# A streaming encoder layer: the last product as seven block products in a stage of its own

## The chip, the cores and the metric

The kernel runs on one core of one Trainium2 chip. Its time is the device time of one execution in microseconds; the kernel before takes 1970.81 us, the median of three runs (1968.71 to 1971.21). A profile is one further execution, recorded by the hardware. Engines are named as in the profile: PE is the matrix engine and PEld its weight load, DVE the vector engine, ACT the scalar (activation) engine, POOL the general engine, SP the queue that issues the DMAs.

## What is computed

One layer of a hybrid encoder, on 2048 prompt frames and 64 sample frames, with a model width of 1024. Attention with 4 heads (branch A, "diff") and retention with 4 heads (branch B, "ret") each give an output of width 512 per frame. The part that matters here is what follows them:

```python
def layer_output(x, oa, ob, za, zb, ga, gb, subln_g, lam_init, w_oa, w_ob, w_out):
    B, T = x.shape[0], x.shape[1]
    oa = (rmsnorm(oa, subln_g) * (1.0 - lam_init)).reshape(B, T, W_A) * jax.nn.silu(za)
    ob = rmsnorm(ob).reshape(B, T, W_B) * jax.nn.silu(zb)
    m = ga * (oa @ w_oa) + gb * (ob @ w_ob)
    return x + m @ w_out
```

`ga` and `gb` are sigmoids of projected inputs plus a bias. `oa @ w_oa` and `ob @ w_ob` are 512 to 1024 each, and are called the branch products here; `m @ w_out`, 1024 to 1024, is the last product. All inputs and outputs are float32.

## The kernel before, in words

A float32 product is made of three products of a rounded format: each operand is split into a high part (`h`, a cast on ACT) and a low part (`l`, what the cast left out, a subtraction on DVE or POOL), and the sum h·h + h·l + l·h is accumulated in a PSUM bank.

The program is written by a planner. The work is a set of Python generators ("tasks") with priorities; a loop takes the most urgent one that can go on by a model of the engines' times (`P`, `A`, `V`, `G` for PE, ACT, DVE and POOL, `ld` and `st` for DMAs), and the instructions of PE, ACT and DVE stand in exactly the order in which the tasks emit them. Every DMA is issued on SP, in emission order as well. A task that yields a time waits in the model only; on the chip an instruction waits for the data and buffers that it needs. `take` and `give` count buffers of a tag (`BUFS`).

Two streams fill most of the time: input projections (`w_stream`) and attention with retention (`z_stream`). They leave in DRAM the branch outputs (`oaT`, `obT`), the branch gates (`zaT`, `zbT`) and the merge gates before their sigmoid (`gaT`, `gbT`), all transposed, with channels on the partitions, in eight groups of 264 columns (256 prompt frames and 8 sample frames, `GW`).

The last stage (`out_stream`) goes through the eight groups. For a group, `m_tile` makes for each of eight channel tiles (`ct`) the branch product of A in a bank `mm` and of B in a bank `s`, 12 matmuls each with 264 columns (lines 1685 to 1687); `m_fin` multiplies each by its gate (line 1704), adds the two on POOL (1708), splits the sum into high and low tiles that stay in SBUF (1714, 1717), and copies out the sample columns (1723). Then `y_tile` makes the last product of two blocks of 128 frames: for each half of the output channels 24 matmuls with 512 columns (1758 to 1760) into a bank `at`, and `y_fin` adds `x` and stores (1791). The sample frames' product (1754) stands before the last block. `og_fin` makes the operands `ogh`, `ogl` of the branch products: POOL multiplies `on` by `z`, ACT takes the sigmoid of `z`, DVE multiplies by it. `gate` loads `gt` and takes its sigmoid on ACT. `load_wo` and `load_wout` bring the weights and split them.

Of the kernel before, what the change touches and what calls it, by code (L numbers as in the profile page):

```python
# [16 lines left out]
T = 2048  # L17
# [18 lines left out]
        "oz": 11, "og": 16, "gt": 8, "wst": 4, "m": 16, "xt": 2, "yt": 2}  # L36
# [8 lines left out]
EARLY = 3  # L45
# [17 lines left out]
class Hybrid:  # L63
    def __init__(self, tc, ins, outs):
# [9 lines left out]
        self.live = {"z": 0, "w": 0, "r": 0}  # L74
# [80 lines left out]
    def scratch(self):  # L155
# [13 lines left out]
        self.obT = tc.dram_tile([4, 128, 8 * GW], F32, name="obT")  # L169

    def consts(self):
# [33 lines left out]
        nc.vector.tensor_scalar_mul(self.gsub, self.gsub, 0.8)  # L205
# [1201 lines left out]
    def ret_block(self, k, t0, r, first):  # L1407
# [88 lines left out]
        nc.vector.tensor_scalar(ms, ms, 1.0 / 128, EPS, op0=ALU.mult, op1=ALU.add)  # L1496
# [69 lines left out]
    def load_wo(self, q):  # L1566
        sl = slice(256 * q, 256 * q + 256)
        for br, name in enumerate(("w_o_diff", "w_o_ret")):
            for kt in range(4):
                h, l, slot = self.wo[br][kt]  # L1570
                yield from self.take("oz")
                s = self.sb(self.z3, [128, GW], "oz", "wst")[:, :256]
                t = self.ld(s, self.i[name][0, 128 * kt:128 * kt + 128, sl], 1 << 17)
                self.spawn(self.split_fin("oz", h[:, sl], l[:, sl], s, t, (kt + q) % 3 == 0, slot, q), 2)
                yield self.pe

    def load_wout(self):
        pool = self.z4
        for ct in range(8):
            h = pool.tile([128, 1024], F32R, tag=f"woh{ct}", name=f"woh{ct}")  # L1580
            l = pool.tile([128, 1024], F32R, tag=f"wol{ct}", name=f"wol{ct}")
            self.wout.append((h, l, {}))
        for nh in range(2):
            sl = slice(512 * nh, 512 * nh + 512)
            for ct in range(8):
                h, l, slot = self.wout[ct]
                k = 8 * nh + ct
                tag = ("xt", "xt", "yt", "yt")[k] if k < 4 else "wst"
                yield from self.take(tag)
                s = self.sb(pool, [128, 512], tag, "wst")  # L1590
                t = self.ld(s, self.i["w_out"][0, 128 * ct:128 * ct + 128, sl], 1 << 18)
                self.spawn(self.split_fin(tag, h[:, sl], l[:, sl], s, t + 600, False, slot, nh), 2)
                self.wout_left -= 1
                yield self.pe

    def out_prep(self):
        pa = self.z3
        for br, name in enumerate(("w_o_diff", "w_o_ret")):
            for kt in range(4):
                h, l = (pa.tile([128, 1024], F32R, tag=f"{name}{n}{kt}", name=f"{name}{n}{kt}") for n in "hl")  # L1600
                self.wo[br].append((h, l, {}))
        yield from self.load_wo(0)
        for g in range(8):
            gsl = slice(GW * g, GW * g + GW)
            for br, (oT, zT) in enumerate(((self.oaT, self.zaT), (self.obT, self.zbT))):
# [10 lines left out]
            if g == 0:  # L1616
                for ct in range(EARLY):
                    yield from self.take("oz", 2)
                    pair = [self.sb(pa, [128, GW], "oz", "gt") for _ in range(2)]
                    self.spawn(self.gate(ct, pair, "oz"), 1)  # L1620
                for q in range(1, 4):
                    yield from self.load_wo(q)
                yield lambda: self.wout_left == 0

    def og_fin(self, on, z, t, og):
        nc = self.nc
        yield t
        nc.gpsimd.tensor_mul(on, on, z)
        t = self.G(GW, self.pe)
        yield t  # L1630
# [381 lines left out]
```

## Time and profile before

| what | value |
|---|---|
| median of three runs | 1970.81 us |
| profiled execution, first to last instruction | 1970.5 us |
| first branch product (line 1685) | 1588.4 us |
| last matmul ends near | 1966.8 us |
| PE busy | 1954.8 us (99%) |
| DVE, ACT, POOL busy | 1048.8, 993.2, 418.9 us |
| DMA issued on SP | 283.85 MB, 49.0% of the 16 engines' span |

A window row of the profile has, behind its stretch and its length, the busy time of each engine with its number of instructions in brackets, then the granted PE clock as a share, the mean busy share of the 16 DMA engines, and GB/s. A row of the timeline has start, duration, engine, line, operation, tiles and count. A row of a group of instructions has the busy time, the mean duration of one in ns, and then the idle time before them with what ended it. A row of DMA issues has the count, the size of one and the median time from issue to landing.

### The profile page before, as it was taken

How to read it: one execution, taken by the hardware profiler on the slowest of the kernel's cores; microseconds unless marked ns; L12 is line 12 of the kernel's file. 1: busy time of each engine (PE TensorE's matmuls, PEld its weight loads, DVE VectorE, ACT ScalarE, POOL GpSimd, SP SyncE). 2: the span in 40 equal slices, each digit the busy share in tenths (PEclk: the TensorE clock that was granted, in tenths of full speed). 3: DMA queues.
4: the chain of work that ended last, by engine and by line, in shares of the span. 5: the costliest groups of instructions: out<-in, count | busy, mean ns of one | idle time of the engine just before them, and what ended most of it. 6: DMA issues, size and time to landing. Idle time of an engine off the chain costs nothing. (4 is left out here: it accounts for less than half of the span.)

```text
span 1970.5 us, 34013 instructions
## 1 busy us (share of the span) xinstructions
PE 1954.8 (99%) x12158; PEld 1753.9 (89%) x12158; DVE 1048.8 (53%) x2795; ACT 993.2 (50%) x2190; POOL 418.9 (21%) x387
## 2 busy tenths in 40 slices
PE   9999999999999999999999999999999999999999
PEld 7878999999988989999998888888888888888997
DVE  6553665536555236547757656635753356444433
ACT  6432776655544436436756666635654554333321
POOL 2310211212111121212112112112112434222210
PEclk9999999999999999999999999999999999999999
DMA  7647554336655656664352342553234666444432
GB/s 245 212 129 195 152 158 122 110 89 164 180 162 166 163 158 194 189 198 148 105 144 92 97 134 78 160 148 97 65 94 130 197 215 205 145 134 136 140 94 60
DMA packets 332429, 286.03 MB, mean 145 GB/s; under 512 B 65250, under 2 KB 296930, under 8 KB 332259
## 3 DMA queue, kind: packets, MB, share of 16 engines
q1 hardware_dynamic: 332258, 283.85, 49.0%
q8 instruction: 96, 1.57, 0.4%
q14 instruction: 75, 0.61, 0.1%
HBM read 187.22 MB, written 91.49 MB: 141 GB/s over the span
## 5 line engine op out<-in xcount | busy, mean ns | idle before, releaser
L516 PE MATMUL mm<-xh,wh 128*128 128x512 f32 (+2 forms) x1280 | 459.1, 359 | 0.0
L516 PE MATMUL mm<-xh,wl 128*128 128x512 f32 (+2 forms) x1280 | 452.3, 353 | 0.0
L516 PE MATMUL mm<-xl,wh 128*128 128x512 f32 (+2 forms) x1280 | 451.7, 353 | 0.0
L480 POOL TENSOR_TENSOR wl<-ws,wh 128x512 fp32r<-128x512 f32 x189 | 257.0, 1372 | 814.9 <-ACT wh L470 629.5
L516 PEld LDWEIGHTS mm<-xh,wl 128*128 128x128 f32 x1280 | 241.0, 188 | 31.6
L516 PEld LDWEIGHTS mm<-xh,wh 128*128 128x128 f32 x1280 | 241.3, 189 | 29.0 <-issue 0.2
L516 PEld LDWEIGHTS mm<-xl,wh 128*128 128x128 f32 x1280 | 241.6, 189 | 27.9
L516 PE MATMUL mm<-wh,xh 128*128 128x256 f32 (+1 forms) x824 | 258.4, 314 | 1.2 <-DVE tlo L753 1.0
L516 PE MATMUL mm<-wh,xl 128*128 128x256 f32 (+1 forms) x824 | 253.4, 308 | 0.0
L516 PE MATMUL mm<-wl,xh 128*128 128x256 f32 (+1 forms) x824 | 253.1, 307 | 0.1
L1119 DVE TENSOR_TENSOR atl<-at,ath 128x512 fp32r<-128x512 f32 (+1 forms) x144 | 93.8, 660 | 162.6 <-ACT ath L1117 162.6
L810 ACT COPY ev<-mm 128x512 f32<-128x512 f32 x140 | 71.5, 511 | 194.1 <-PE mm L516 166.0
L516 PEld LDWEIGHTS mm<-wh,xh 128*128 128x128 f32 x824 | 156.7, 190 | 10.9 <-DVE tlo L753 1.4
L516 PEld LDWEIGHTS mm<-wl,xh 128*128 128x128 f32 x824 | 156.9, 190 | 9.2 <-POOL wl L480 0.3
L516 PEld LDWEIGHTS mm<-wh,xl 128*128 128x128 f32 x824 | 156.7, 190 | 8.0
L1035 ACT ACTIVATE row<-row,a_mx 128x1024 f32<-128x1024 f32 (+7 forms) x160 | 153.9, 963 | 12.9 <-DVE a_mx L1015 12.6
L1005 DVE CUSTOM_DVE_ANT_0 row<-s,dfar 128x512 f32<-128x512 f32 (+2 forms) x192 | 118.6, 631 | 54.5 <-PE s L997 54.0
L470 ACT CAST wh<-ws 128x512 fp32r<-128x512 f32 x192 | 116.2, 619 | 44.8 <-PE mm L516 18.5
L1117 ACT CAST ath<-at 128x512 fp32r<-128x512 f32 (+1 forms) x144 | 79.0, 564 | 104.8 <-PE at L1104 97.4
L996 PE MATMUL s<-K,q 128*128 128x512 f32 (+3 forms) x320 | 118.7, 374 | 1.4 <-DVE a_acc L1005 1.4
L997 PE MATMUL s<-K,q 128*128 128x512 f32 (+3 forms) x320 | 115.2, 363 | 0.4 <-DMA q<-qT 0.4
L1057 DVE SCALAR_TENSOR_TENSOR row<-row,a_w 128x1024 f32<-128x1024 f32 (+4 forms) x96 | 103.6, 1086 | 14.4 <-ACT row L1054 14.1
(238 smaller groups left out, 4036.1 us busy)
## 6 DMA issues: line engine op xcount, KB each, us to landing
ws<-in_w_in_dram SPq DMA_DIRECT2D x192, 256.0 KB, 3.0
q<-qT SPq DMA_DIRECT2D x128, 128.0 KB, 3.1
V<-vN SPq DMA_DIRECT2D x24, 512.0 KB, 5.5
K<-kT SPq DMA_DIRECT2D x48, 256.0 KB, 4.2
gt<-gaT SPq DMA_DIRECT2D x64, 132.0 KB, 2.1
gt<-gbT SPq DMA_DIRECT2D x64, 132.0 KB, 2.2
xt<-in_x_prompt_dram SPq DMA_DIRECT2D x16, 512.0 KB, 6.1
kn<-in_cache_k_T_dram SPq DMA_DIRECT2D x32, 256.0 KB, 3.7
```

The source lines that it names most:

```text
L470: self.nc.scalar.copy(h, st)
L480: self.nc.gpsimd.tensor_sub(l, st, h.bitcast(F32))
L516: nc.tensor.matmul(ps, p, q, start=c == 0 and i == 0, stop=c == KC - 1 and i == 2)
L810: nc.scalar.copy(ev, ps)
L996: nc.tensor.matmul(ps, q1s, kk, start=True, stop=False)
L997: nc.tensor.matmul(ps, q2s, kk, start=False, stop=True)
L1005: nc.vector.tensor_tensor_reduce(out=units[k0 // 1024][:, k0 % 1024:k0 % 1024 + n], in0=ps, in1=tab, scale=-SLOPES[h], scalar=3.0e38, op0= ...
L1035: nc.scalar.activation(u, u, AF.Exp, bias=mx, scale=-1.0, accum_out=lp[:, k:k + 1])
L1057: nc.vector.scalar_tensor_tensor(out=u0, in0=u0, scalar=w[:, 0:1], in1=u1, op0=ALU.mult, op1=ALU.add)
L1117: nc.scalar.copy(ah[:, :w], at[:, :w])
L1119: nc.vector.tensor_sub(al[:, :w], at[:, :w], ah[:, :w].bitcast(F32))
```

## The change

*Seven block products.* For 256 prompt frames the last product is seen as a product of 2 by 2 blocks: two frame blocks of 128, two halves of the inner dimension, two halves of the output channels. In place of eight block products it makes seven (P1 to P7), of sums and differences of blocks, and adds them up in the order of Winograd's form. A block product is 12 matmuls with 512 columns. `b_prep` builds the seven blocks of weights (three blocks of `w_out` as they are, four sums `t1` to `t4`), `y_prep` the blocks of `m` (`a11`, `a12`, `a22` and the sums `s1` to `s4`) for each group, on DVE, POOL and ACT; `y_group` emits the products, several into the same bank one after another, and `y_out` takes the intermediate sums T, U, V out of the banks with ACT, adds `x` to them on POOL, and adds the banks on DVE.

*A stage of its own, one branch at a time.* Before, the branch products and the last product of a group followed each other. Now the branch products of A go through all eight groups, then those of B, then all last products. Between them the tiles go through DRAM: `m_fin` of A stores its gated tile to `uaT`; for B it is loaded again (`ua`), added on POOL, and the sum is stored to `mT`, from which `y_prep` and `y_sample_in` load.

*Gates.* `og_fin` uses the Silu function on ACT and one multiplication on POOL, in place of POOL, sigmoid on ACT, and DVE. The merge gate is a tanh of half the argument; 1 is added in the multiplication itself (line 1695), and the factor of one half is put into constants ahead (`gsub`, `bg`, the retention's norm).

How rows of the order stand, with line, operation, tile written and tiles read, and the shape. On SP, the queue of the DMAs, in the last stage of before, from one group to the next (`gt` are gates, `oxt` the input `x`, `oyt` the output):

```order
L138 DMA gt<-gaT 128x264
L138 DMA gt<-gbT 128x264
L138 DMA z<-zbT 128x264
L138 DMA on<-obT 128x264
L138 DMA z<-zbT 128x264
L143 DMA out_y_prompt_dram<-oyt 128x512
L138 DMA oxt<-in_x_prompt_dram 128x512
L138 DMA on<-obT 128x264
L143 DMA out_y_prompt_dram<-oyt 128x512
L138 DMA oxt<-in_x_prompt_dram 128x512
```

and in the change, in the branch products of B:

```order
L146 DMA mT<-gt 128x264
L141 DMA z<-zbT 128x264
L141 DMA on<-obT 128x264
L141 DMA z<-zbT 128x264
L141 DMA on<-obT 128x264
L141 DMA z<-zbT 128x264
L141 DMA on<-obT 128x264
L146 DMA mT<-gt 128x264
L141 DMA ua<-uaT 128x264
L141 DMA gt<-gbT 128x264
L141 DMA ua<-uaT 128x264
L141 DMA gt<-gbT 128x264
```

To the gate's load came, for each channel tile, a load `ua` and a store `mT`; in the products of A a store `uaT` came. From the first `uaT` store to the last one there are 207 DMAs, and from there to the last `mT` store 232.

On SP, where the branch products end and the block products begin:

```order
L146 DMA mT<-gt 128x264
L141 DMA a<-mT 128x4x128 x2
L141 DMA oxt<-in_x_prompt_dram 128x512 x8
L141 DMA sm<-mT 128x8x8 x8
L141 DMA oxt<-in_x_prompt_dram 128x512
L146 DMA out_y_prompt_dram<-u 128x512
```

The last store of `mT` is followed by the rest of group 1's blocks (`a`), eight loads of `x`, and the eight loads of the sample's columns (`sm`). On ACT at the same place, where `u` are the sums T, U, V, `ah` high parts of the blocks (three for group 0, then seven for group 1), and `smx` the sample's high part:

```order
L1655 ACTIVATE gt<-gt,bg 128x264 x12
L1874 COPY u<-mm 128x512
L1786 CAST ah<-a 128x512 x3
L1874 COPY u<-mm 128x512
L1874 COPY u<-at 128x512
L1913 CAST smx<-sm 128x8x64
L1786 CAST ah<-a 128x512 x7
```

The sample's cast stands ahead of all of group 1's casts; on DVE the sample's subtraction stands ahead of group 1's sums in the same way.

The diff, cut to its core:

```diff
 BUFS = {...
-        "oz": 11, "og": 16, "gt": 8, "wst": 4, "m": 16, "xt": 2, "yt": 2}
+        "oz": 10, "og": 16, "gt": 8, "ua": 3, "st": 8, "wa": 8, "wb": 8, "ac": 12, "u": 9, "xt": 8}
+BLOCKS = ("11", "21", "22", "t1", "t2", "t3", "t4")
+PAIRS = {"P1": ("a11", "11"), "P6": ("s2", "t2"), "P2": ("a12", "21"), "P7": ("s3", "t3"),
+         "P5": ("s1", "t1"), "P4": ("a22", "t4"), "P3": ("s4", "22")}
+HOME = {"a11": "wb", "s2": "wb", "a12": "wb", "s3": "wb", "s1": "ac", "a22": "ac", "s4": "ac"}
...
+    def gates(self):
         for br, gT in enumerate((self.gaT, self.gbT)):
+            for n in range(64):
+                g, ct = divmod(n, 8)
+                gsl = slice(GW * g, GW * g + GW)
+                yield from self.take("gt")
+                gt = self.sb(self.z3p, [128, GW], "gt")
+                ua = None
+                if br:
+                    ut = "wb" if self.has("wb") else "ua"
+                    yield from self.take(ut)
...
+                    self.ld(ua[0], self.uaT[ct][:, gsl], 1 << 17)
+                t = self.ld(gt, gT[ct][:, gsl], 1 << 17)
+                self.spawn(self.gate(br, g, ct, gt, ua, t), 0)
+                yield self.pe
...
+    def m_fin(self, br, g, ct, ps, tag, t):
+        nc = self.nc
+        yield lambda: (br, g, ct) in self.gts
+        gt, ua, tg = self.gts.pop((br, g, ct))
+        t = max(t, tg)
+        yield t
+        nc.vector.scalar_tensor_tensor(out=gt, in0=gt, scalar=1.0, in1=ps, op0=ALU.add, op1=ALU.mult)
+        t = self.V(GW, t)
+        self.give(tag, t)
+        if br:
+            yield t
+            nc.gpsimd.tensor_add(gt, gt, ua[0])
+            t = self.G(GW, t)
+            self.give(ua[1], t)
+        yield t
+        t = self.st((self.mT if br else self.uaT)[ct][:, GW * g:GW * g + GW], gt, 1 << 17)
+        self.give("gt", t)
+        if br:
+            self.mt[g].append(t)
...
+    def y_prep(self):
+        for g in range(8):
+            yield lambda: len(self.mt[g]) == 8
...
+                t = self.ld(raw[k], self.mT[4 * kh:4 * kh + 4, :, c0:c0 + 128].rearrange("c p t -> p c t"), 1 << 18)
...
+            for step in (hi("a11"), sm("s1", False, ALU.add, "a21", "a22"), hi("a12"), sm("s2", False, sub, "s1", "a11"),
+                         sm("s3", True, sub, "a11", "a21"), hi("s2"), sm("s4", True, sub, "a12", "s2"), lo("a11"),
+                         lo("s2"), lo("a12"), hi("s3"), lo("s3"), hi("s1"), hi("a22"), lo("s1"), hi("s4"), lo("a22"),
+                         lo("s4")):
+                yield from step
...
+    def y_group(self):
+        for g in range(8):
+            seq += [(g, "P1"), (g, "P2"), (g, "P6")] if g == 0 else [(g, "P6"), (g, "P2")]
+            seq += [(g, "P5"), (g, "P7")]
+            seq += [(g + 1, "P1")] if g < 7 else []
+            seq += [(g, "P3"), (g, "P4")]
+        bank = {"P1": "a", "P6": "a", "P7": "a", "P4": "a", "P2": "b", "P5": "c", "P3": "c"}
+        tags = {"a": "mm", "b": "s", "c": "at"}
+        after = {"P6": "T", "P7": "U", "P4": "C22", "P3": "V"}
...
+            for c in range(4):
+                wh, wl, t = self.wt[kb][c]
+                for m, (u, v) in enumerate(((ah[:, c], wh), (ah[:, c], wl), (al[:, c], wh))):
+                    nc.tensor.matmul(q[b], u, v, start=fresh and c == 0 and m == 0, stop=c == 3 and m == 2,
+                                     skip_group_check=True)
...
+    def y_sample_in(self):
+        s = self.z6.tile([128, 8, 64], F32, tag="sm", name="sm")
+        m = self.z6.tile([128, 8, 2, 64], F32R, tag="smx", name="smx")
+        for ct in range(8):
+            t = self.ld(s[:, ct].rearrange("p (g c) -> p g c", c=8),
+                        self.mT[ct].rearrange("p (g c) -> p g c", c=GW)[:, :, 256:GW], 1 << 15)
+        yield t + 3000
+        nc.scalar.copy(m[:, :, 0], s)
+        nc.vector.tensor_sub(m[:, :, 1], s, m[:, :, 0].bitcast(F32))
...
     def out_stream(self):
-        for g in range(8):
-            og = []
-            for ct in range(8):
-                yield from self.m_tile(g, ct, og)
-            for tt in range(2):
-                if g == 7 and tt:
-                    yield from self.y_tile(7, None, 64, self.i["x_sample"][0], self.o["y_sample"][0])
...
+        for br in range(2):
+            for g in range(8):
+                og = []
+                for ct in range(8):
+                    yield from self.m_tile(br, g, ct, og)
+            if br == 0:
+                self.ma_end = self.pe + LAT
+                self.give("wb", self.ma_end, 8)
+        self.spawn(self.y_open(), 0)
+        yield from self.y_group()
+
+    def y_open(self):
+        yield lambda: self.live["m"] == 0
+        self.z3.close()
+        self.z6 = self.es.enter_context(self.tc.tile_pool(name="p3y", bufs=1, side="right"))
+        for k in ("ac", "u", "xt"):
+            self.give(k, self.pe, BUFS[k])
+        self.spawn(self.y_x(), 0)
+        self.spawn(self.y_sample_in(), 1)
```

`y_open` gives the memory of the branch stage (`z3`) to the block stage (`z6`: `u`, `oxt`, `sm`, the blocks of kind `ac`).

468 lines of the change are left out of this document (275 added, 193 removed).

## The prediction

> **What bounds the kernel now.** I read the page first, then the windows of the last stage, then the queue that issues its DMAs. The page's head:
>
> ```profile
> span 1970.5 us, 34013 instructions
> PE 1954.8 (99%) x12158; PEld 1753.9 (89%) x12158; DVE 1048.8 (53%) x2795; ACT 993.2 (50%) x2190; POOL 418.9 (21%) x387
> ```
>
> TensorE (PE) is busy 99% of the span at the full granted clock, so a kernel that takes matmuls away gains exactly their time, unless something else becomes late. All of the change lies behind 1588.4 us, where the first product with `ogh` starts. The windows of that stage, cut where PE goes from branch products (m) to last products (y), for groups 2 and 3; then the sample's product, and the whole stage:
>
> ```profile
> core 0: us, PE busy (x) PEld busy (x) DVE busy (x) ACT busy (x) POOL busy (x), PEclk, DMA share, GB/s
> 1683.30:1706.70 23.40, 23.40 (x194) 23.40 (x193) 10.64 (x36) 9.12 (x25) 5.38 (x7) 1.00 0.38 117
> 1706.70:1729.30 22.60, 22.52 (x99) 17.93 (x98) 10.37 (x25) 6.35 (x16) 7.20 (x9) 1.00 0.55 165
> 1948.00:1955.50 7.50, 7.46 (x32) 5.26 (x33) 2.07 (x3) 0.00 (x0) 0.00 (x0) 1.00 0.52 157
> 1588.40:1966.80 378.40, 376.15 (x2337) 335.81 (x2335) 178.23 (x487) 129.12 (x319) 99.97 (x122) 1.00 0.47 141
> ```
>
> A group of 256 tokens has 192 branch matmuls in 23.4 us (0.122 each; 12 of them, one channel tile of one branch, are 1.46) and 96 last matmuls in 22.6 us (0.235 each); the sample's 32 take 7.5 us (0.234). Eight times 46.0 plus 7.5 is 375.5 of the stage's 378.4 us: PE hardly waits. The DMA engines are half used, and SP, the one queue that issues every DMA, is idle most of the time. Behind the last matmul come an addition and a store; the chain's end:
>
> ```profile
> 1966.56 0.25 PE at L1760
> 1966.83 0.69 DVE oyt L1791
> ```
>
> From 1966.8 to the end at 1970.5 are 3.7 us.
>
> **Part 1, fewer matmuls.** In the order of the changed program the last product has 672 instead of 768 matmuls of the same shape (84 for 96 per group); the sample has 40 by its loops (16 and 24) instead of 32. The branch matmuls are the same 1536. So PE needs 8 x 23.4 + 672 x 0.235 + 40 x 0.234 = 187.2 + 158.2 + 9.4 = 354.8 us for what took 378.4: 23.6 us less. If PE never waited, the profiled execution would go from 1970.5 to 1946.9.
>
> **Part 2, the detour through DRAM.** Before, a gated tile stayed in SBUF. Now every one of the 64 tiles of branch A is stored (`uaT`), loaded again for branch B, and the sum stored (`mT`); the gate loads and the `on`/`z` loads stay. Counted in the order of SP: from the first `uaT` store to the last `mT` store there are 439 DMAs (207 to the last `uaT` store, 232 behind it), where the branch products of before had some 32 per group. They meet PE time of 127 tiles x 1.46 = 185.7 us. What an issue costs is seen where SP has nothing to wait for:
>
> ```profile
> 1754.41 0.32 SPq L138 DMA_DIRECT2D gt<-gbT  x1
> 1754.83 0.38 SPq L138 DMA_DIRECT2D on<-oaT  x1
> ...
> 1760.06 0.38 SPq L138 DMA_DIRECT2D z<-zbT  x1
> 1593.22 3.94 SPq L138 DMA_DIRECT2D wst<-in_w_out_dram  x8
> ```
>
> Twelve issues from 1754.41 to 1760.06 are 0.471 us each (the durations of 0.32 to 0.38 leave out the step to the next), eight of twice the bytes in 3.94 us 0.49 each. I take 0.474. Then SP needs 438 x 0.474 = 207.6 us between the first and the last store: **21.9 us more than PE**. In branch A that is 207 issues, 98 us against 94; in branch B 3.6 per tile, 1.72 us against 1.46. SP's rows are in a fixed order, so a late SP makes gates late, gates hold the four PSUM banks of the branch products, and PE waits. Nothing hides this: it takes back nearly all of part 1.
>
> [...]
>
> The other side of the same bytes: the 439 DMAs move 62.1 MB (132 KB for 408 of them). The fullest stretches before:
>
> ```profile
> 1539.00:1546.00 7.00, 7.00 (x33) 5.79 (x32) 2.53 (x4) 5.51 (x12) 4.80 (x7) 1.00 0.99 297
> 1590.00:1605.00 15.00, 15.00 (x125) 15.00 (x124) 11.74 (x24) 10.09 (x22) 4.98 (x6) 1.00 0.86 278
> ```
>
> At share 0.99 the engines move 297 GB/s, so 62.1 MB need 209 us: the same size as the issue time. SP also keeps eight completion semaphores in turn, so an issue waits until the DMA eight before it has landed; at 0.474 that is 3.8 us, and these are the landing times:
>
> ```profile
> gt<-gaT SPq DMA_DIRECT2D x64, 132.0 KB, 2.1
> on<-obT SPq DMA_DIRECT2D x32, 132.0 KB, 3.1
> oxt<-in_x_prompt_dram SPq DMA_DIRECT2D x32, 256.0 KB, 3.4
> rqk<-kbT SPq DMA_DIRECT2D x16, 256.0 KB, 4.5
> gaT<-ev SPq DMA_DIRECT2D x8, 32.0 KB, 3.1
> ```
>
> Mostly below 3.8, so I put the waits in this stage at +3 us (1.5%); at the worst mixed burst before, stores among loads, an issue took 0.52 us, from the first to the last of these eight steps:
>
> ```profile
> 1639.43 0.32 SPq L138 DMA_DIRECT2D on<-obT  x1
> ...
> 1643.58 0.37 SPq L138 DMA_DIRECT2D gt<-gaT  x1
> ```
>
> That is the upper bound: 438 x 0.52 = 227.8. The lower one is 438 x 0.46 = 201.5 (a little below any run of eight issues here).
>
> **Part 3, from branch products to block products.** The first tile ends at 1589.9; with its gating (0.43, and hand-overs)
>
> ```profile
> L1704 DVE TENSOR_TENSOR gt<-s,gt 128x264 f32<-128x264 f32 x64 | 27.5, 430 | 35.2 <-PE s L1687 35.0
> ```
>
> the first store is at about 1590.6, the last at t = 1590.6 + 207.6 = 1798.2. PE is up to four banks ahead of it and begins P1 and P2 of group 0 before t. P6 of group 0 adds to P1's bank, so first ACT copies that bank into a tile `u`, whose memory the last store frees when it has landed, at about t + 2.2 (`gt<-gaT`'s 2.1 is the nearest row for the size); with 0.6 for the copy P6 starts near t + 3, and P6, P5, P7 of 2.82 each end near t + 11.6. Then P1 of group 1 is due. Its operands come from `mT` late: ACT casts `smx`, and DVE subtracts it, before they come to group 1, and `sm` stands on SP behind eight `oxt` loads, which wait for the memory of the branch stage, so for the last store to land (t + 2.2). Eight issues: t + 6; eight `sm` issues of 32-byte pieces, like `gaT<-ev` of 32 KB, at some 0.57: t + 10; landing 3.1: t + 13. Then by the nearest operations
>
> ```profile
> L1554 ACT CAST woh<-wst 128x512 fp32r<-128x512 f32 x16 | 9.7, 617 | 2.7 <-DMA wst<-in_w_out_dram 2.5
> L1561 DVE TENSOR_TENSOR wol<-wst,woh 128x512 fp32r<-128x512 f32 x16 | 10.9, 688 | 2.6 <-ACT woh L1554 2.6
> L480 POOL TENSOR_TENSOR wl<-ws,wh 128x512 fp32r<-128x512 f32 x189 | 257.0, 1372 | 814.9 <-ACT wh L470 629.5
> L1708 POOL TENSOR_TENSOR gt<-gt 128x264 f32<-128x264 f32 x64 | 53.5, 837 | 152.8 <-DVE gt L1704 78.0 <-DVE ms L1723 72.0 <-DMA wst<-in_w_out_dram 2.7
> ```
>
> one cast (0.62) and four DVE steps (`smx`, two sums, the first low part; 2.75) follow: P1 of group 1 starts at t + 17, a wait of 5 us (bounds: 0, if `sm` lands early, and 9, if loads of 4.5 us do).
>
> **Part 4, the block stage itself.** Per group PE has 84 x 0.235 = 19.8 us. Beside it lie: DVE 13 operations of 0.69 = 9.0; ACT 7 casts and 3 copies of 0.62 = 6.2; POOL 5 of 1.37 = 6.9; SP 12 issues = 5.7, 3 MB, 155 GB/s. All fit at least twice on their engines, and the bank hand-overs have two products (5.6 us) between them; I allow 2 us of waits in all (0 to 7). In the branch stage POOL has 0.84 per tile of branch B and half of
>
> ```profile
> L1628 POOL TENSOR_TENSOR on<-on,z 128x264 f32<-128x264 f32 x56 | 45.3, 814 | 95.7 <-DMA on<-obT 43.6 <-DMA on<-oaT 33.7 <-DVE ms L1723 5.7
> ```
>
> for `on`, 1.25 of SP's 1.72. Silu and tanh change no count of table loads (two in either order). Removed casts and copies were idle time's work: no gain.
>
> **Sum.** t + 17 = 1815.2; 51 products of 12 matmuls, 51 x 2.82 = 143.8; the sample 9.4; tail 3.7: 1972.1. With 3 and 2 for waits: **1977 us**, +6.5 on the profiled 1970.5. That execution stands 0.3 below the median of 1970.81, so the forecast of the median is 1977 as well: slower by 0.3%. A measurement here tells about 0.2%, 3.9 us, from no change.
>
> **Rivals.**
> *A, SP keeps up: faster.* The place is SP's queue in branch B. Issues that stand between waits cost 0.42, as single ones do (1754.41 to 1754.83); 438 x 0.42 = 184 is below PE's 185.7 us. Then the time is 1946.9 plus the transition of 5 and 2 of waits: 1954. It decides from about 0.45 us per issue downwards. [...] Against it: every run of eight or more issues that the trace has is at 0.46 or above.
> *B, the lag is there and the transition is not:* PE, four banks ahead, and `sm`, small, hide it: 1972.1 - 5 + 3 = 1970, no change. For it: the bounds of part 3 go down to 0. Against it: the row order on SP and ACT.
> *C, the engines and the eight semaphores bind too:* 0.52 per issue, 1972.1 + 20.2 = 1992. For it: 297 GB/s at share 0.99, against 296 GB/s wanted without a break for 210 us. Against it: 1754 to 1760, twelve issues without a wait.
> That the seven products do not save matmuls is excluded by the order of PE.
>
> **How the numbers follow.** Forecast 0.55, A 0.15, B 0.15, C 0.15. The forecast's own range is 1971 to 1986 (0.471 to 0.49 per issue, 0 to 7 of waits); about 0.13 of its 0.55 lies below 1974.7 and counts as no change. The low end of A and the top of C are left out: 1960 to 1995. Faster 0.15 + 0.02 from B = 0.17; same 0.13 + 0.13 + 0.02 = 0.28; slower 0.42 + 0.13 = 0.55.
>
> **What would show it.** SP issuing without a break, 0.47 us apart, from about 1600 to 1798; the weight loads' (PEld) busy share, full in branch products now, near 0.9 there, PE's waits ended by DVE's gating; last `mT` store near 1798 and the last matmul near 1973; block groups at 20 us. Wrong if the branch stage ends before 1785 (A), if PE has no gap behind P7 of group 0 (B), if issues stand 0.5 us or more apart (C), or if block groups take over 21 us: then part 4's cover fails.

## The result, and the profile after

The changed kernel takes **2014.5 us** (median; 2013.3 to 2015.9) beside 1970.3 us before (median of four here): the ratio is 1.0227, 95% interval 1.0213 to 1.0242. The forecast was 1977 us with a range from 1960 to 1995. The side was right, the size was not: 44 us lost instead of 6. The page of the changed kernel, its head and the DMA rows that answer to those of before:

```profile
span 2013.8 us, 34306 instructions
PE 1955.2 (97%) x12070; PEld 1751.0 (87%) x12070; DVE 1040.5 (52%) x2641; ACT 1024.3 (51%) x2219; POOL 466.5 (23%) x427
...
gt<-gaT SPq DMA_DIRECT2D x64, 132.0 KB, 3.2
uaT<-gt SPq DMA_DIRECT2D x64, 132.0 KB, 3.2
ua<-uaT SPq DMA_DIRECT2D x64, 132.0 KB, 3.3
gt<-gbT SPq DMA_DIRECT2D x64, 132.0 KB, 3.3
```

PE is busy 97% of a longer span, although it has fewer matmuls, and the gates' loads land in 3.2 us where they took 2.1. The windows of the last stage, cut at the first and last store of `uaT`, the last store of `mT`, and a stretch of block products:

```profile
core 0: us, PE busy (x) PEld busy (x) DVE busy (x) ACT busy (x) POOL busy (x), PEclk, DMA share, GB/s
1591.10:1708.60 117.50, 105.08 (x801) 102.31 (x799) 64.19 (x139) 64.00 (x149) 25.98 (x31) 0.96 0.84 253
1708.60:1834.30 125.70, 105.28 (x744) 98.28 (x744) 48.90 (x102) 52.21 (x118) 68.29 (x87) 0.96 0.88 258
1861.50:1984.00 122.50, 122.50 (x530) 99.39 (x529) 50.58 (x81) 33.60 (x61) 40.47 (x31) 1.00 0.48 145
```

The block products run as forecast: PE never waits in 122.5 us. The loss is in the first two rows. The stores take from 1591.1 to 1834.3, **243.2 us**, where the prediction had 207.6 + 3; the granted clock is 0.96. What PE waited for, from the first branch product on:

```profile
PE mm L1677 <- DVE gt L1695: 20.1, 16, 3.8
PE s L1677 <- DVE gt L1695: 11.8, 16, 2.2
PE mm L1846 <- ACT ah L1786: 5.5, 1, 5.5
PE mm L1846 <- ACT u L1874: 3.6, 1, 3.6
PE mm L1846 <- DVE al L1793: 2.0, 1, 2.0
```

(us in total, times, longest.) In the branch products PE waits for banks that DVE's gating has not emptied (L1695). One link further back, on ACT, the tanh of the gates in the stretch from 1600 to 1825:

```profile
ACT gt L1655 <- DMA gt<-gbT: 51.0, 47, 3.2
ACT gt L1655 <- DMA gt<-gaT: 29.7, 27, 4.2
```

ACT waited 81 us in 74 places for the gates' loads to land, DVE for ACT, PE for DVE. And SP, which issues those loads, waited in its turn for products and stores:

```profile
SPq L141 <- POOL gt L1700: 6.7, 15, 0.9
SPq L146 <- DVE gt L1695: 4.1, 5, 3.0
SPq L146 <- DVE ogl L1630: 3.8, 9, 1.2
SPq L146 <- POOL gt L1700: 3.8, 7, 1.1
SPq L141 <- DVE gt L1695: 3.3, 7, 1.1
SPq L141 <- DMA uaT<-gt: 3.2, 7, 0.8
```

From SP's issue times in the trace: the median step between two issues is 0.476 us, as forecast (0.474), but 56 steps of the 438 are over 0.6 us and add 34 us, 19 in branch A and 15 in branch B. 438 x 0.476 + 34 = 242.5, the 243 of the stores. Of the 42 us of waits that the profile lists for SP between the first and the last store, 31 end with work of DVE, POOL and ACT, and 11 with the landing of an earlier DMA: 9.0 of these in branch A, the weights' 4.8 first (`wst`, from `in_w_out`).

These weights, in loads of 256 KB, stand behind PE's longest waits as well. Three waits, of 3.3, 3.8 and 3.5 us (up to 1649.2, 1680.5 and 1744.5), each come down to a gate's load that was issued 0.5 to 2.5 us behind the last of four such loads, weights for the seven blocks in branch A and blocks of group 0 (`a`) in branch B. It took 4.9, 6.1 and 4.3 us to land, where the median is 3.2. The second of them, on SP and then on ACT:

```profile
1670.90 1.91 SPq L141 DMA_DIRECT2D wst<-in_w_out_dram  x4
1672.91 0.38 SPq L146 DMA_DIRECT2D uaT<-gt  x1
1673.33 0.43 SPq L141 DMA_DIRECT2D gt<-gaT  x1
1679.50 0.51 ACT L1655 ACTIVATE gt<-gt,bg 128x264 f32<-128x264 f32 x1 [4.17 <-DMA gt<-gaT]
```

No run moves these loads, so what they cost by themselves is not shown.

PE's side of the same stage, from the starts of its 1536 branch matmuls: 1589.0 to 1827.3, 238.3 us. Of the 1535 steps, 1376 are under 0.2 us (median of all steps 0.122), 37 are waits of 0.3 us or more and lie 38.3 us above plain steps, and 122 take 0.2 to 0.3 us, 12.3 us above plain steps. 1535 x 0.122 + 38.3 + 12.3 = 237.9. Of the slow steps 82 stand in five runs of 12 to 26, which are a half clock, shown below; the others follow single waits.

### The profile page after: what moved, and what is told of

Same layout as the page of the kernel before. It is cut to its first block, busy times and chain, and to the rows that moved or that the text cites. A ratio compares the mean times of both kernels' runs of the same rounds, so it can differ in the third digit from the quotient of the medians.

```text
span 2013.8 us, 34306 instructions
## 1 busy us (share of the span) xinstructions
PE 1955.2 (97%) x12070; PEld 1751.0 (87%) x12070; DVE 1040.5 (52%) x2641; ACT 1024.3 (51%) x2219; POOL 466.5 (23%) x427
## 4 chain that ended last, share of the span: by engine, by line
PE 82%; DMA 8%; SPq 3%; DVE 3%; issue 2%; ACT 1%; POOL 1%; POOLq 0%; ACTq 0%; DVEq 0%
PE mm L522 50%; PE mm L1846 4%; PE s L1002 3%; PE s L1003 3%; PE at L1110 3%; SPq L141 2%; PE at L1846 2%; PE pv L1090 2%; PE pv L1089 2%; PE pv L1088 2%; DMA gt<-gbT 2%; DMA gt<-gaT 1%; PE s L1846 1%; DMA qT<-thi 1%; PE pv L1471 1%
## 5 line engine op out<-in xcount | busy, mean ns | idle before, releaser
L1655 ACT ACTIVATE gt<-gt,bg 128x264 f32<-128x264 f32 x128 | 64.9, 515 | 106.5 <-DMA gt<-gbT 55.2
## 6 DMA issues: line engine op xcount, KB each, us to landing
q<-qT SPq DMA_DIRECT2D x128, 128.0 KB, 3.0
```

The source lines that it names most:

```text
L1655: self.nc.scalar.activation(gt, gt, AF.Tanh, scale=0.5, bias=self.bg[:, br, ct:ct + 1])
```

## The experiments

The stage's time here is from the first to the last start of the branch matmuls in each run's profiled execution. "Halves" are the first and the last 64 of its 128 tiles; where branch A goes first, the first half is A. PE alone needs 93.6 us for each. The medians are of two executions for split loads and six gate buffers, of four to ten for the others. All runs without the detour but the first have the sample rows late as well.

| run | median us | ratio to before (95% interval) | stage | halves |
|---|---|---|---|---|
| changed kernel | 2014.5 | 1.0227 (1.0213-1.0242) | 238.3 | 112.3, 126.1 |
| gates alone, on before | 1969.2 | 0.9997 (0.9987-1.0006) | - | - |
| no detour | 1972.0 | 1.0008 (0.9999-1.0018) | 197.4 | 99.9, 97.4 |
| sample rows late | 2008.3 | 1.0200 (1.0184-1.0217) | 238.6 | 111.9, 126.7 |
| both of these | 1968.0 | 0.9988 (0.9976-1.0000) | 197.8 | 99.7, 98.0 |
| z, on issued by ACT | 2015.8 | 1.0232 (1.0217-1.0247) | 237.2 | 117.6, 119.6 |
| short pieces | 2004.4 | 1.0177 (1.0160-1.0194) | 228.3 | 104.0, 124.3 |
| these two | 1996.6 | 1.0129 (1.0106-1.0152) | 219.3 | 105.0, 114.3 |
| split loads | 2050.3 | 1.0408 (1.0387-1.0429) | 272.0 | 128.0, 144.0 |
| pair loads | 2010.3 | 1.0207 (1.0189-1.0225) | 234.9 | 111.0, 123.8 |
| pair loads, short pieces | 1993.0 | 1.0116 (1.0099-1.0133) | 219.3 | 102.4, 116.9 |
| + 11 gate buffers | 1985.4 | 1.0076 (1.0060-1.0093) | 213.1 | 97.2, 115.9 |
| + sums loaded in pairs | 1974.3 | 1.0021 (1.0011-1.0031) | 207.9 | 99.2, 108.7 |
| six gate buffers | 2022.5 | 1.0268 (1.0248-1.0289) | 245.9 | 116.4, 129.5 |
| 12 gate buffers | 2066.9 | 1.0487 (1.0471-1.0504) | 265.6 | 114.9, 150.7 |
| planner's clock | 2019.1 | 1.0250 (1.0233-1.0267) | 245.0 | 116.0, 129.0 |
| no detour, planner's clock | 1971.7 | 1.0007 (0.9997-1.0016) | 201.5 | - |
| no detour, pair loads | 1982.5 | 1.0065 (1.0050-1.0080) | 209.8 | 110.0, 99.8 |
| no detour, z and on spread | **1965.6** | **0.9976 (0.9967-0.9985)** | 194.9 | 97.3, 97.6 |

### Are the gates to blame?

The kernel before, with the changed kernel's silu and tanh and nothing else:

```diff
-    nc.scalar.activation(z, z, AF.Sigmoid)
+    nc.scalar.activation(z, z, AF.Silu)
...
-    nc.vector.tensor_mul(gs[br], ps, gs[br])
+    nc.vector.scalar_tensor_tensor(out=gs[br], in0=gs[br], scalar=1.0, in1=ps, op0=ALU.add, op1=ALU.mult)
```

> The kernel before, with nothing but the new gates (silu in place of multiply, sigmoid, multiply; tanh with the half scale and a fused multiply in place of sigmoid and multiply). If the gates carry none of the loss: 1966-1973 us, within 0.2 per cent of before. If a good part of the 44 us comes from ACT's or DVE's new operations: 1980 us or more.

1969.2 us, no difference. The gates carry none of the loss.

### Is the detour to blame?

Branch A and branch B of each group one after the other. A's tile waits in SBUF for B's, so the 64 stores and 64 loads of `uaT` are gone:

```diff
-    for br in range(2):
-        for g in range(8):
+    for g in range(8):
+        for br in range(2):
...
-        if br:
-            yield t
-            nc.gpsimd.tensor_add(gt, gt, ua[0])
+        if br == 0:
+            self.uas[g, ct] = gt
+            return
+        yield t
+        nc.gpsimd.tensor_add(gt, gt, self.uas.pop((g, ct)))
```

> The whole computation, with branch A and branch B of each token group one after the other instead of all of A and then all of B: branch A's product waits in its gate tile (13 gate buffers, z and on 8) for branch B's, and the 64 stores to the scratch tensor and the 64 loads from it are gone. 311 issues on SP x 0.476 us = 148 us and 45 MB instead of 62 (151 us at 297 GB/s) then both lie under PE's 187 us. If the detour over DRAM is the cause: stage 188-200 us, kernel 1966-1980 us. If the loss sits in one branch after the other as such (gates, weights, order of the work on ACT and DVE): stage 220 us or more, kernel 1998 us or more.

1972.0 us, 42.5 below the changed kernel, and the stage has 41 of them. So the loss goes with the detour. The stage's window there:

```profile
1586.80:1784.20 197.40, 189.82 (x1537) 187.62 (x1536) 110.34 (x230) 110.95 (x258) 95.19 (x118) 1.00 0.75 220
```

against the changed kernel's

```profile
1589.00:1827.30 238.30, 206.28 (x1536) 198.13 (x1535) 112.24 (x238) 115.56 (x266) 91.27 (x114) 0.96 0.86 256
```

The same matmuls cost PE 190 us of busy time instead of 206: the clock stays at 1.00. The edit changes five things at once, though: issues, bytes, a chain through the DRAM, a tight pool (13 gate buffers instead of 8 and 3), and the order of the branches. The next runs take the first four apart. The order, all of A before all of B, stays in them, and the last of them ("sums loaded in pairs") has a stage 10.5 us longer than this one, so that up to so much of the 41 may be the order's.

### Issues or bytes?

First the loads of `z` and `on` from ACT's queue, then the detour's DMAs shortened to 8 columns (the sum then leaves out branch A but for these columns; POOL adds the gate's tile to itself in its place), then both:

```diff
-    self.ld(z, zT[kt][:, gsl], 1 << 17)
+    self.ld(z, zT[kt][:, gsl], 1 << 17, self.nc.scalar)
```
```diff
-    self.ld(ua[0], self.uaT[ct][:, gsl], 1 << 17)
+    self.ld(ua[0][:, :8], self.uaT[ct][:, GW * g:GW * g + 8], 1 << 17)
...
-    t = self.st((self.mT if br else self.uaT)[ct][:, GW * g:GW * g + GW], gt, 1 << 17)
+    t = self.st(self.uaT[ct][:, GW * g:GW * g + 8], gt[:, :8], 1 << 17)
```

> The changed kernel, with the 128 loads of z and on in the branch stage issued by ACT and not by SP; bytes, buffers and order otherwise as they were. SP then has 311 DMA issues left in the stage instead of 439. Theory I (SP's issue time bounds the branch stage, and its waits add to it since it can bank nothing): 311 x 0.476 us = 148 us is less than PE's 187 us, so the stage between the first and the last branch product falls from 238 us to 190-205 us and the kernel to 1970-1985 us. Theory T (the 62 MB of transfers, their landing times of 3.3 us and the eight completion semaphores bound it): the same bytes and the same number of transfers, the stage stays at 225 us or more and the kernel at 2000-2015 us.

> The changed kernel, with the store of branch A's product and its load cut to the first 8 of 264 columns of each tile (32 bytes a row instead of 1056), as many DMAs as before; the branch sum thus leaves out branch A but for these columns, so the output is not the whole one. Some 17 of 62 MB are gone from the branch stage. Theory I (issue time on SP): 439 x 0.476 us = 209 us of issues are left, the stage stays at 209-238 us and the kernel at 1985-2014 us. Theory T (bytes and engines): at the bytes moved per microsecond that the changed kernel shows, 45 MB take 0.73 of the time, so PE's 187 us bound the stage and the kernel comes to 1963-1975 us.

> The two edits of the first runs together: the loads of z and on issued by ACT, and the store and load of branch A's product cut to 8 of 264 columns (so the output leaves out branch A but for these columns). Alone they took 0 and 10 us. Theory J (two resources were each near full in the branch stage, SP with 439 x 0.476 = 209 us of issues and the DMA engines with 62 MB or 209 us at 297 GB/s, so that taking one load away leaves the other): with both gone the stage between the first and the last branch product falls from 238 us to 190-203 us and the kernel to 1970-1985 us. Rival B (the eight gate buffers: a tile's cycle of load, tanh, product, store and the store's landing is too long, whatever the queues carry): the stage stays at 215 us or more and the kernel at 1995 us or more.

0, 10 and 18 us less. By its numbers the first run speaks for T, the second for I (a quarter of the bytes gone, and the time stays in I's range), the third for B. They agree only if the first edit is no clean relief, and its waits show that. A load that ACT issues stands between the tanhs in ACT's order; the time from a gate load's issue to its tanh in branch A rose from 3.2 to 6.9 us (mean over tiles 17 to 64). SP, free of 95 issues between the first and the last store (344 instead of 439), waited more than before, now for the landing of stores:

```profile
SPq L141 <- DMA uaT<-gt: 27.0, 30, 3.2
```

which was 3.2 us in 7 places. In branch A 28 of 48 gate loads (tiles 17 to 64) went out within 0.25 us of the landing of the store from the same buffer, 7 in the changed kernel. So SP has an issue time that is nearly full and, behind it, a second limit at almost the same place: the gate buffers. Then the issue time by itself, up and down, without another queue:

```diff
-    t = self.ld(on, oT[kt][:, gsl], 1 << 17)
+    self.ld(on[:64], oT[kt][:64, gsl], 1 << 16)
+    t = self.ld(on[64:], oT[kt][64:, gsl], 1 << 16)
```
```diff
-    for kt in range(4):
+    for kp in range(2):
...
+        self.ld(z, zT[2 * kp:2 * kp + 2, :, gsl].rearrange("c p t -> p c t"), 1 << 18)
```

> The changed kernel, with each of the 64 loads of on split in two by partitions: 64 more issues on SP (503 x 0.476 us = 239 us), same bytes and packets. Theory I: the stage grows by 64 x 0.476 = 30 us less what SP idles now, 255-268 us, kernel 2031-2045 us. Theory T: SP's added time lies in its idle time of 30 us, 238-245 us, 2014-2022 us.

> The changed kernel, with z and on loaded for two row blocks at once: 64 DMAs of 264 KB instead of 128 of 132 KB, same bytes and packets, same buffer space (5 pairs instead of 10), all on SP. 64 issues x 0.476 us = 30 us less on SP, 375 issues or 178 us. Theory I (SP's issues set the pace): the stage falls from 238 us to 205-218 us, the kernel to 1982-1996 us. Theory T (the DMA engines with 62 MB): 230 us or more, 2006-2016 us. In between (each nearly full, the other takes over): 218-230 us.

Up: the stage grew by 33.7 us, more than theory I had (255 to 268 us), and the DMA engines were less busy for it. Of the 64 issues more, 48 lie between the first and the last store (487 DMAs there). A whole load of `on` takes 0.51 us to the next issue, on average; the two halves take 0.52 and 0.71, so 48 x 0.72 = 34.6 us. Why the second half's step is longer than an ordinary 0.476 is open. The stage's window:

```profile
1589.60:1861.60 272.00, 213.39 (x1537) 202.94 (x1535) 113.34 (x238) 116.46 (x266) 89.10 (x114) 0.94 0.76 224
```

So what is added to SP's time comes out in the stage in full; engines with a quarter of their time free did not hide it. Down: 64 issues fewer, 43 of them between the first and the last store (43 x 0.476 = 20.5 us), gave 3.4 us, with the engines at 0.88:

```profile
1586.70:1821.60 234.90, 201.74 (x1537) 194.75 (x1535) 112.97 (x239) 116.16 (x272) 94.08 (x119) 0.97 0.88 266
```

That is theory T's number: I is right in one direction only. Pairs also make the buffers coarser: in the version without the detour, where SP is not short, the same edit cost 12 us of stage:

> The version without the detour and with the late sample rows (1968 us), with pair loads of z and on: 247 issues instead of 311. If SP's bursts cause the 10 us that PE waits in its branch stage of 198 us: 1960-1966 us, below the kernel before. If the waits come from the order on ACT and DVE or from buffers: 1966-1971 us.

1982.5 us, outside both expectations and 14.5 slower than without pairs; the longest waits are two for `ogh`, 8.4 us together, one of them 7.0 us at the first tile of a group. What fewer issues are worth by themselves may thus be more than 3.4 us; it was not measured apart.

### The turn of a gate buffer

In branch A of the changed kernel (tiles 17 to 64, by the order of the loads, tanhs, gatings and stores in the trace) one gate buffer's turn is, on average: 3.2 us from the load's issue to its tanh, 0.5 tanh, 0.3 until DVE, 0.4 gating, 6.0 until its store is through SP's queue, and 4.7 until the next load in that buffer is issued; from load to load 15.4 us. Eight buffers at 15.4 us make a tile every 1.93 us; PE needs 1.46. A gate's load is issued 1.7 tiles ahead of its gating; at PE's 1.46 us a tile that is 2.5 us, less than its landing time of 3.2. In 41 of the 48 tiles the product itself, which goes ahead into one of four banks, has already begun by then.

Of these, the 6.0 us until the store is through are time in SP's queue, so fewer and more buffers were tried:

```diff
- "oz": 10, "og": 16, "gt": 8, "ua": 3
+ "oz": 8, "og": 16, "gt": 12, "ua": 1
```
```diff
- "gt": 8,
+ "gt": 6,
```

> The changed kernel with 12 buffers for gate tiles instead of 8; the room comes from the loads of z and on (8 buffers instead of 10) and the extra ones for branch A's product (1 instead of 3). Issues and bytes as they were. Theory B (gate buffers are too few to ride over SP's bursts): the stage falls from 238 us to 210-222 us, near SP's 209 us, and the kernel to 1988-2000 us. Theory J (SP and the DMA engines full): 230 us or more, 2006-2016 us.

> The changed kernel with 6 buffers for gate tiles instead of 8, nothing else. In the first half of the stage a buffer's turn (load, tanh, product, SP's queue, store, landing) is 15.4 us on average in the changed kernel, which is 8 x 1.93 us, where PE needs 1.46 us a tile. Theory B (that turn sets the pace): of the 15.4 us some 8-9 us are landings and engine work that don't shrink, so a tile takes 1.6 to 2.5 us in place of 1.9 and the kernel is slower by 10-60 us, 2025-2075 us. Theory J (issues and bytes set the pace, the turn only fills up the time there is): 2010-2020 us.

Six buffers cost 8 us, between the two expectations (2022.5 us, where theory B had 2025 or more and J 2020 or less): the wait in SP's queue fell from 6.0 to 2.9 us, and the rest of the turn grew instead. Twelve made it 52 us slower, which none had expected. In branch A 7.5 us then passed from a gate's tanh to its gating (0.3 in the changed kernel), so the buffers were enough, and the half was none the shorter (114.9 us). Gatings whose gates were ready stood, in DVE's order, behind the subtractions for `ogl`, which waited for ACT's casts; from 1590 to 1700:

```profile
DVE ogl L1630 <- ACT ogh L1627: 16.4, 5, 5.9
```

where it was 4.5 us in 2 places. In branch B `z`, with two buffers less for it and `on`, was waited for more,

```profile
ACT z L1616 <- DMA z<-zbT: 23.1, 21, 4.0
```

where it was 8.3 us. With one `ua` tile instead of three, too, branch B took 150.7 us and the transition 26 us more. As a test of buffers alone the run is not clean. A clean one needs room: with short pieces the `ua` tiles are 8 columns wide, and that room makes three more gate buffers. On top of pair loads and short pieces came 11 gate buffers, and on top of these the loads of branch A's (short) product for two tiles at once:

```diff
- "oz": 5, "og": 16, "gt": 8, "ua": 3
+ "oz": 5, "og": 16, "gt": 11, "ua": 3
...
-    self.sb(self.z3p, [128, GW], ut), ut)
+    self.sb(self.z3p, [128, 8], ut), ut)
```
```diff
-    self.ld(ua[0][:, :8], self.uaT[ct][:, GW * g:GW * g + 8], 1 << 17)
+    if ct % 2 == 0:
...
+        self.ld(up.rearrange("p (c t) -> p c t", c=2),
+                self.uaT[ct:ct + 2, :, GW * g:GW * g + 8].rearrange("c p t -> p c t"), 1 << 17)
```

> Pair loads of z and on and the store and load of branch A's product cut to 8 of 264 columns (branch A is left out of the sum but for these columns): 375 issues or 178 us on SP, 45 MB or 151 us of engine time, both under PE's 187 us. Theory J (SP and engines together): stage 190-203 us, kernel 1968-1982 us. If the chain from a store's landing to the next gate load in the same buffer sets the pace by itself: 212 us or more, 1990 us or more.

> The run with pair loads and short pieces (1993 us, stage 219 us; branch A is left out of the sum but for 8 of 264 columns of each tile) with 11 gate buffers instead of 8, in the room that branch A's short product leaves. In that run a buffer took 13.2 us from one load to the next, 8 x 1.66 us, where PE needs 1.46 us a tile. Theory R (the buffers' turn holds it: the next load stands behind the store's landing): with 11 buffers the turn allows 1.2 us a tile, so PE sets the pace, stage 190-205 us, kernel 1964-1980 us. If the order of the loads and of the work on ACT and DVE holds it: 214-224 us, 1988-1998 us.

> The run with pair loads, short pieces and 11 gate buffers (1985 us, stage 213 us: 96 in the first half, 115 in the second; branch A is left out of the sum but for 8 of 264 columns), with the loads of branch A's product taken for two tiles at once: 32 issues less, all in the second half, which then has about 168 x 0.476 = 80 us of issues. If SP's issues hold the second half: 96-106 us there, kernel 1966-1977 us. If the chain of loads, tanh, product and sum or the order on ACT and DVE holds it: 110 us or more, 1980-1988 us.

Pair loads and short pieces together came to a stage of 219.3 us: not J's 190 to 203, but what its rival had, the chain over a store's landing. With 11 buffers the first half came down from 102.4 to 97.2 us, close to PE's 93.6: gate loads now went out 4.9 tiles ahead of their gating. There theory R holds. The second half hardly moved (116.9, 115.9), so stage and kernel (213.1, 1985.4) lie between the two expectations. With 32 issues fewer there it fell to 108.7, between the two expectations, and the kernel by 11 us, to a time that the first of them had. Taken in turn from 238.3 us: bytes 10.0, issues 9.0, buffers 6.2, issues again 5.2; 20.7 us above PE's 187.2 are left, against 10 without the detour.

So the loss has no single owner. Each of three limits, SP's issues (209 us), the DMA engines (share 0.86) and the buffers' turn, was close enough to the stage's time to take over from another. The shares hold for this order of the edits alone. What of the second half's last 15 us is SP and what the chain of load, tanh, product and sum, stays open.

### The order on the engines

After the run with 12 buffers another theory stood: that the planner, which counts 0.44 us for a 128 KB load and nothing for a store, sets work that waits for late loads ahead of the gating. Its DMA clock was set to 0.476 us for each DMA from the branch stage on:

```diff
-    self.dma = max(self.dma, self.pe) + nbytes / 300.0
+    self.dma = max(self.dma, self.pe) + max(nbytes / 300.0, self.issue)
...
+    if self.issue:
+        self.dma = max(self.dma, self.pe) + self.issue
```

> The changed kernel, with the planner's clock of the DMA queue set, from the branch stage on, by what the trace shows: each DMA on SP, stores too, takes at least 476 ns there (the planner counts 0.44 us for a 128 KB load and nothing for a store). Only the order in which the instructions are laid out on the engines changes. Theory O (in the planner's order, work that waits for late loads stands ahead of gates' products on the in-order queues of ACT and DVE, which is why 12 gate buffers did not help): the stage falls from 238 us to 215-230 us, the kernel to 1990-2007 us. Theory J (SP's issues and the DMA engines full, in whatever order): 235-243 us, 2010-2020 us.

> The kernel without the detour and with the late sample rows (1968 us, stage 198 us, of which PE works 187), with the same clock of the DMA queue in the planner. Theory O: the waits of some 10 us in the stage halve, 1958-1966 us, below the kernel before. Otherwise no difference, 1965-1971 us.

Both got slower, by 4.6 and 3.8 us. So this other order is no better, and theory O as it was put falls; that the order on DVE and ACT can bind is seen in the run with 12 buffers, and what a better one would give is not shown.

### The transition

```diff
     def y_sample_in(self):
+        yield lambda: "T" in self.yq[3]
```

> The changed kernel, with the nine loads of the sample rows and the cast and subtraction on them put off until the first product of prompt group 3 has been copied, out of the transition. Theory of the transition as predicted (sample loads and casts stand ahead of group 1's on SP, ACT and DVE): the first product of group 1 starts 3-6 us sooner after the last store than the 20 us of the changed kernel, and the kernel gets 3-6 us shorter, 2008-2012 us. Rival (the chain from the last store over the loads and sums of group 1 sets it whatever the sample does): no change, 2013-2016 us.

> The kernel of the run without the detour, with the sample rows' loads and casts put off until the first product of prompt group 3 as well. That alone took 6 us off the changed kernel. If the two losses are separate they add up: 3-7 us below the run without the detour, 1961-1975 us, which may be below the kernel before. If group 0 and 1's weights and rows are late for another reason once the branch stage is short: no gain over the run without the detour.

2008.3 us, 6.2 below the changed kernel; without the detour 4.1. PE's waits for the block products in the first:

```profile
PE mm L1846 <- ACT u L1874: 3.8, 1, 3.8
PE mm L1846 <- DVE al L1793: 3.4, 1, 3.4
```

The 5.5 us for `ah` ahead of group 1's P1 are gone (P1 starts 13.2 us behind the last store, not 20.2): the sample's cast and loads in front of group 1's made it, as part 3 had it. The wait for `al` inside P1 is 3.4 us instead of 2.0.

### A version that beats both

Without the detour and with late sample rows, the loads of `z` and `on` are also held back to 16 tiles ahead of their product:

```diff
+    yield lambda: self.nt >= 2 * len(self.ogs) - 16
     yield from self.take("oz", 2)
```

> The version without the detour and with the late sample rows (1968 us, stage 198 us), with the loads of z and on held back so that no pair is issued more than 16 tiles ahead of its product. If early z and on loads push the gates' loads back in SP's queue: stage 190-195 us, 1960-1965 us. Otherwise 1966-1972 us.

```profile
span 1962.7 us, 34014 instructions
PE 1936.8 (99%) x12070; PEld 1738.5 (89%) x12070; DVE 1050.0 (53%) x2641; ACT 1020.2 (52%) x2219; POOL 472.1 (24%) x427
```

1965.6 us: 0.24% faster than before (0.15 to 0.33%), and 2.4% faster than the changed kernel. The time lies between the two expectations, the stage, 194.9 us, at the edge of what the first theory had; the 2.3 us below the run with both edits are not clear of the noise. Of the 23.6 us that the seven products save, 7.7 go to PE's waits in the stage (194.9 against 187.2) and 11.9 to the transition (its first twelve products take 45.3 us, 12 x 2.785 = 33.4 without waits).

## Why the prediction was wrong, point by point

- **Part 1, 23.6 us of matmuls: right.** From the 13th block product on there is none that waits; each takes 2.785 us (2.82 forecast).
- **Part 2, the issue time: right.** 439 DMAs, 0.476 us a step, 0.474 forecast.
- **Part 2, "I put the waits in this stage at +3 us": this step failed.** They were 34. The allowance rested on landing times of before, mostly below 3.8 us, taken as if they stayed so. Beside a DMA share of 0.86 the gates' rose from 2.1 to 3.2 us; that is still below 3.8, but the rows compared left out the weights, which at 256 KB took 5.0 us, and landings ended 11 of SP's 42 us of waits. The other 31 were in no term: the prediction had PE wait for SP, but not SP for PE and its gatings. SP's stores and buffers wait for products whose gates SP itself loads a little earlier: with gates 1.7 tiles ahead of their gating each end of that loop waits for the other, and what SP loses it can't make up, since its issues alone (209 us) take longer than PE's work (187). The upper bound of 0.52 us an issue, 227.8 us, fell short too: it came from a burst of eight in the kernel before, in whose last stage SP is idle most of the time. That is nearly the whole of the miss: by the last `mT` store 33.1 of the 36.7 us between the forecast's sum (1977.1) and the profiled execution (2013.8) have come.
- **Part 2, the rates of PE in that stage:** 0.122 us a matmul held for 1376 of 1535 steps. The half clock behind long waits, some 8 us by the 82 steps (0.22 for 0.122), was in no term.
- **Rival C, engines and semaphores bind as well:** the nearest in time, with 1992 us, and right in part. Its sign of 0.5 us between issues didn't come by the median (0.476) and did by the mean (0.555). The eight semaphores are seen to bind: in the changed kernel's trace the 1662 DMAs carry eight semaphores in strict turn, and none was issued before the one eight ahead of it had landed, where the landing is seen; the store issued at 1677.42 us waited 1.9 us for the weights' load eight issues before it, out at 1671.37 and landed at 1677.36. But landings are 11 of 42 us.
- **Part 3, the transition: right in its mechanism.** P6 of group 0 began at the last store + 3.3 us (3 forecast), P1 of group 1 waited 5.5 us (5) and started at + 20.2 (17). Most of the 3 us between are P6 at half clock, 5.3 us instead of 2.8.
- **Part 4, waits of 2 us:** one of 2.0 for `al`, inside P1 of group 1; POOL and DVE kept up.
- **A and B** fell: SP did not keep up, and P7 of group 0 had the gap behind it.

## What to carry to other kernels

Where a queue's issue time comes out as near to the work it feeds as here (209 us beside 187), don't add a small allowance for waits: look at how far ahead of its use each load is issued. Here that lead was 2.5 us beside a landing time of 3.2, and 34 us of waits came on top of SP's issues where 3 were allowed. The detour over DRAM cost its issues, its bytes and the buffers that wait for its landings; shorter pieces alone gave 10 us of the 44 back, pair loads alone 4. A change of loop order that keeps the tile on the chip gave back 42 of the 44 us with as many buffers as before, 13 for gates and 8 for `z` and `on` instead of 8, 10 and 3. Look at what stands just ahead of a load that is needed soon, too: behind four loads of twice the size a gate's load landed after 4.3 to 6.1 us here, where the median is 3.2.

## What the runs showed of the hardware

**The clock halved behind a wait of 2.2 us, and not behind one of 2.4.** One of the stretches at half clock in the changed kernel, first PE's rows and then the windows around it:

```profile
1676.45 0.28 PE L1679 MATMUL s<-ogh,woa 128*128 128x264 f32 x1
1680.53 0.59 PE L1677 MATMUL mm<-ogh,woa 128*128 128x264 f32 x1 [3.79 <-DVE gt L1695]
1680.92 0.42 PE L1678 MATMUL mm<-ogl,woa 128*128 128x264 f32 x1
1681.14 0.42 PE L1679 MATMUL mm<-ogh,woa 128*128 128x264 f32 x1
```

```profile
1676.00:1680.00 4.00, 0.74 (x7) 0.53 (x5) 0.69 (x1) 0.50 (x2) 0.00 (x0) 0.99 0.90 310
1680.00:1686.80 6.80, 6.27 (x29) 6.27 (x29) 5.35 (x10) 4.15 (x10) 1.63 (x2) 0.51 0.84 239
```

For 6.8 us a matmul started every 0.22 us instead of 0.122. In the last stage the changed kernel has seven such stretches, of 3.4 or 6.8 us, five of them in the branch products and two in the transition (34 us at half clock), each in or behind a wait of 2.2 to 5.5 us; before had none, and the branch products of the version of 1965.6 us have a granted clock of 1.00. So a wait here cost itself and up to half of the next 3.4 or 6.8 us. The shortest of these waits: behind 2.23 us without a matmul, from 1775.3 to 1777.5, the clock was at half from 1778.9 to 1782.3. Behind 2.39 us, from 1767.3 to 1769.7, it stayed at 1.00. The changes of the clock lie a multiple of 3.41 us apart; on that grid the first wait fell into one window but for 0.2 us, and the second into two, 1.4 and 1.0 us. Two cases make no rule, and what sets the clock is not shown.

**An issue cost the same for 4 KB as for 132 KB.** With the short pieces SP's median step stayed at 0.475 us (0.476 in the changed kernel) while the DMA share of the stage fell from 0.86 to 0.69, so shorter transfers relieved the engines and not the queue; 264 KB in one DMA cost no double step either: behind the pair loads the median steps, tile by tile, were 0.49 to 0.57 us. Longer were the 0.71 us behind the second half of a split load, and in the changed kernel six of the eight steps of the sample loads (`sm`, 32 KB in pieces of 32 bytes), 0.71 to 0.85 us; the other two, 2.5 and 3.0 us, were longer still.
